# Products within a chunk of a bidirectional RWKV-7 scan: four 64x64 TensorE tiles in place of block-diagonal weights

## The chip, the core and the metric

The kernel runs as one program on one NeuronCore of a Trainium2 chip. The metric is the device time of one execution in microseconds (us). Three runs of the kernel before took 1759.25, 1768.68 and 1767.44 us; their median is 1767.44 us.

## The reference, cut to what matters

One layer mixes 128 context tokens and 2048 latent tokens. Eight heads of 64 channels go through RWKV-7 time mixing, once forwards and once backwards; the other half of the width is a short gated convolution. Projections stand before both and one output projection behind them. Only the scan matters here:

```python
def step(S, inp):
    r_t, w_t, k_t, v_t, kk_t, a_t = inp
    s_kk = jnp.einsum('bdhij,bdhj->bdhi', S, kk_t)
    S = (S * w_t[..., None, :] - s_kk[..., :, None] * (kk_t * a_t)[..., None, :]
         + v_t[..., :, None] * k_t[..., None, :])
    return S, jnp.einsum('bdhij,bdhj->bdhi', S, r_t)

s_final, ys = lax.scan(step, s0.astype(f32), xs)
ys = jnp.moveaxis(ys, 0, 2)
y = ys[:, 0] + jnp.flip(ys[:, 1], axis=1)
```

`S` is a 64x64 state for each head and direction. All of it is float32.

## The kernel before, in words

The kernel has three phases whose work overlaps. Phase 1 makes the projections (lines 158 to 160) and writes the scan's operands to memory. Phase 2 is the scan. Phase 3 is the output projection (lines 1219 to 1221).

**Chunks and stages.** The scan is done in chunks of 64 tokens. A pair of heads fills the 128 partitions, since each head has 64 channels. A stage (there are 17, `NST`) works on two groups, one for each direction (`gi` 0 and 1), and each group holds 8 units, a unit being one chunk of one head pair. For one unit the products between the chunk's own operands give four 64x64 blocks for each of the two heads.

**Parts of a stage.** `partL` loads the operands into `rr` (128 partitions: two heads of 64 channels; 5 operands; 8 units; 64 tokens). `partM` makes the products within a chunk: `F` (tile names `psF` in PSUM, `F` in SBUF) and `GA` (`psG`, `GA`), and `Q`, a transpose of one operand (`psQ`). `partI` inverts small triangular blocks on POOL. `partW`, `partU` and `partB` build from these the chunk's matrix `E`: `partU` with 32x32 matmuls (`psU`, `psW`), `partB` with 128x128 matmuls (`psX`, then `psE`). `partS` walks the eight steps of the state: a matmul `psS` of `E` with the state and values `sv`, and a scaling on VectorE that gives the next state. Stage `s`'s `partS` runs together with `partB` of stage `s+1` and `partM` of stage `s+3` (`LA = 3`).

**The products before.** A head pair lies on the 128 partitions, and the two heads must not mix. So `make_bd` (line 766) copies the weight operand into `bd`, a tile of zeros with one head's 64x64 block at the upper right and the other's at the lower left, and one 128x128 matmul gives both heads of one unit (line 829). A group needs two such tiles for each stage, each filled by two copies of 64x512 on ACT: 2 x 2 x 2 groups x 17 stages = 136 copies (line 716 is the helper `copy`). `F` and `GA` are made in halves of four units; a half fills one PSUM bank of 128x512 floats, and VectorE multiplies it by a mask on its way to SBUF (line 830). The pool `pm` has two such banks; `psF`, `psG` and `psQ` take turns in them.

**Slots.** In `F` and `GA` before, the slot number is the unit and the partition half is the head.

**What sets the order.** The code is recorded in the order in which `main` calls the parts. Then a scheduler of the framework goes over it with a timeline of its own and gives each engine a fixed order. TensorE, VectorE and the others run that order one after the other and wait on semaphores. Nothing is reordered between engines at run time by the program.

**How a float32 matmul shows in the trace.** A matmul of float32 is two passes: each is a weight load (PEld) and a matmul (PE) in the trace. So 272 matmuls for `psF` (17 stages x 2 groups x 8 units) show as x544.

## Time and profile before

| what | value |
|---|---|
| median of three runs | 1767.44 us |
| profiled execution, first to last instruction | 1770.7 us |
| PE busy, all matmuls (union) | 1649.1 us, 93% |
| PEld busy, weight loads | 1557.3 us, 88% |
| DVE (VectorE) busy | 1157.2 us, 65% |
| ACT (ScalarE) busy | 831.2 us, 47% |
| POOL (GpSimd) busy | 601.3 us, 34% |
| `psF` and `psG` matmul passes (line 829) | 544 + 544, union 79.7 + 74.7 us |
| copies into `bd` on ACT (line 716) | 136, 83.9 us |

The profiled execution gives no time of its own beside its span; the span is 3.3 us above the median of the runs. The products of `partM` run from 906.6 us to 1476.4 us of the span. A matmul's record in the trace is longer than what it keeps the array busy for, since matmuls are pipelined: the first record's start to the last record's start, divided by the steps between, gives the pace. A row of a timeline merges equal instructions that follow each other: it gives the start of the first, the time to the end of the last, and how many there are.

### The profile page before, as it was taken

How to read it: one execution, taken by the hardware profiler on the slowest of the kernel's cores; microseconds unless marked ns; L12 is line 12 of the kernel's file. 1: busy time of each engine (PE TensorE's matmuls, PEld its weight loads, DVE VectorE, ACT ScalarE, POOL GpSimd, SP SyncE). 2: the span in 40 equal slices, each digit the busy share in tenths (PEclk: the TensorE clock that was granted, in tenths of full speed). 3: DMA queues.
4: the chain of work that ended last, by engine and by line, in shares of the span. 5: the costliest groups of instructions: out<-in, count | busy, mean ns of one | idle time of the engine just before them, and what ended most of it. 6: DMA issues, size and time to landing. Idle time of an engine off the chain costs nothing. (4 is left out here: it accounts for less than half of the span.)

```text
span 1770.7 us, 33010 instructions
## 1 busy us (share of the span) xinstructions
PE 1649.1 (93%) x12400; PEld 1557.3 (88%) x12400; DVE 1157.2 (65%) x2197; ACT 831.2 (47%) x1607; POOL 601.3 (34%) x1089
## 2 busy tenths in 40 slices
PE   5999899999899999999999999899899899899998
PEld 3898899899888999999999989899799899787786
DVE  5998897545777635478843466777677677556333
ACT  4565544224454312255522177667567576433222
POOL 0132210001122100022205528877767868223221
PEclk9999999999899999999999989999899899899999
DMA  9788786564788743478776376767667784645432
GB/s 363 218 244 241 231 253 244 200 237 127 167 193 184 207 153 128 152 191 218 243 249 209 127 178 170 167 178 193 158 172 197 166 193 115 177 149 192 155 129 104
DMA packets 315376, 335.16 MB, mean 189 GB/s; under 512 B 166920, under 2 KB 263560, under 8 KB 301136
## 3 DMA queue, kind: packets, MB, share of 16 engines
q1 hardware_dynamic: 242912, 323.99, 61.5%
q10 hardware_dynamic: 70944, 4.60, 3.0%
q0 software_dynamic: 1360, 4.46, 0.7%
q8 instruction: 98, 1.61, 0.4%
q14 instruction: 62, 0.51, 0.1%
HBM read 221.16 MB, written 111.82 MB: 188 GB/s over the span
## 5 line engine op out<-in xcount | busy, mean ns | idle before, releaser
L871 POOL TENSOR_TENSOR zt<-zt,ztmp 128x30 f32<-128x30 f32 (+7 forms) x510 | 201.9, 396 | 39.7
L987 PE MATMUL psS<-sv,E 128*128 128x64 f32 x1088 | 153.1, 273 | 2.7 <-DVE sv L1000 2.5
L947 PE MATMUL psE<-str,stl 128*128 128x128 f32 x1088 | 149.3, 283 | 5.6 <-ACT str L714 3.8
L987 PEld LDWEIGHTS psS<-sv,E 128*128 128x128 f32 x1088 | 143.3, 197 | 5.9 <-DVE sv L1000 4.3
L947 PEld LDWEIGHTS psE<-str,stl 128*128 128x128 f32 x1088 | 135.0, 196 | 6.9 <-ACT str L714 4.6
L868 POOL TENSOR_TENSOR ztmp<-ab,zt 128x60 f32<-128x60 f32 (+7 forms) x255 | 132.4, 519 | 19.4
L716 ACT COPY bd<-rr 64x512 f32<-64x512 f32 x136 | 83.9, 617 | 90.2 <-issue 35.1
L314 POOL TENSOR_TENSOR shk<-rawl 128x384 f32<-128x384 f32 (+1 forms) x24 | 20.1, 838 | 277.1 <-ACT rawl L310 271.3
L948 DVE TENSOR_TENSOR E<-psE,msk 128x512 f32<-128x512 f32 x136 | 93.4, 687 | 24.3 <-PE psE L947 22.2
L936 PE MATMUL psX<-F,zb 128*128 128x128 f32 x544 | 79.6, 299 | 18.4 <-DVE E L948 13.2
L1000 DVE TENSOR_TENSOR sv<-psS,pc 64x128 f32<-64x128 f32 x254 | 67.9, 277 | 37.3 <-PE psS L987 35.6
L936 PEld LDWEIGHTS psX<-F,zb 128*128 128x128 f32 x544 | 71.8, 209 | 21.7 <-DVE E L948 16.1
L158 PE MATMUL mmv<-h,w 128*128 128x384 f32 (+1 forms) x192 | 70.1, 365 | 19.2 <-ACT q1r L312 10.1
L1282 POOL TENSOR_TENSOR z<-z,x 128x512 f32<-128x512 f32 x32 | 43.7, 1367 | 129.0 <-DVE z L1278 106.8
L829 PE MATMUL psF<-rr,bd 128*128 128x128 f32 x544 | 79.7, 294 | 2.7 <-ACT bd L716 1.8
L829 PE MATMUL psG<-rr,bd 128*128 128x128 f32 x544 | 74.7, 283 | 4.8 <-DVE F L830 4.8
L829 PEld LDWEIGHTS psF<-rr,bd 128*128 128x128 f32 x544 | 71.8, 206 | 3.3 <-issue 2.9
L829 PEld LDWEIGHTS psG<-rr,bd 128*128 128x128 f32 x544 | 68.3, 198 | 5.1 <-DVE F L830 5.0
L195 POOL TENSOR_TENSOR hsls<-sq,hshs 128x384 fp32r<-128x384 f32 (+1 forms) x24 | 31.6, 1318 | 109.5 <-DMA scr_vt<-vt 36.5
L159 PE MATMUL mmv<-h,w 128*128 128x384 f32 (+1 forms) x192 | 68.5, 357 | 0.0
L160 PE MATMUL mmv<-h,w 128*128 128x384 f32 (+1 forms) x192 | 68.0, 354 | 0.1
L158 PE MATMUL mmg<-h,w 128*128 128x384 f32 (+1 forms) x192 | 63.4, 330 | 4.0 <-ACT ta L374 2.0
(308 smaller groups left out, 5193.2 us busy)
## 6 DMA issues: line engine op xcount, KB each, us to landing
w<-scr_wsp SPq DMA_DIRECT2D x68, 1024.0 KB, 6.6
scr_wsp<-w SPq DMA_DIRECT2D x34, 1024.0 KB, 5.6
rr<-scr_ops SPq DMA_DIRECT2D x64, 512.0 KB, 5.0
scr_ops<-sp SPq DMA_DIRECT2D x160, 192.0 KB, 5.1
wr<-in_win SPq DMA_DIRECT2D x34, 512.0 KB, 7.5
ab<-scr_at SPq DMA_DIRECT2D x34, 256.0 KB, 3.8
x<-in_x SPq DMA_DIRECT2D x17, 512.0 KB, 3.7
wadas<-in_wada SPq DMA_DIRECT2D x8, 1024.0 KB, 15.2
```

The source lines that it names most:

```text
L158: T.matmul(ps[:, :n], w[:, 0, k], hh[:, 0, k, :n], start=k == 0, stop=False)
L159: T.matmul(ps[:, :n], w[:, 0, k], hh[:, 1, k, :n], start=False, stop=False)
L160: T.matmul(ps[:, :n], w[:, 1, k], hh[:, 0, k, :n], start=False, stop=k == 7)
L716: (V.tensor_copy if k in ON_DVE else P.copy)(dst, src)
L829: T.matmul(ps[:, i, :].rearrange("p (a b) -> p a b", b=64), w[:, u, :], x[:, :, u, :], start=True, stop=True)
L868: G.tensor_tensor(tv, ab[:, j:j + 2, j + 2:32].unsqueeze(1).broadcast_to((128, kn, 2, n)), zt[:, :kn, j:j + 2].unsqueeze(3).broadcast_to(( ...
L871: G.tensor_tensor(zt[:, :kn, j + 2:32], zt[:, :kn, j + 2:32], tv[:, :, r], ALU.subtract)
L936: T.matmul(px[:, i, :], B.zb[:, gi, us.start + i, :], g.F[:, us.start + i, :], start=True, stop=True)
L947: T.matmul(pe[:, i, hd, :].rearrange("p (b t) -> p b t", b=2), g.lt[:, :, hd, us.start + k + i].rearrange("p b t -> p (b t)"), g.rt[:, :, ...
L948: V.tensor_tensor(g.E[n][:, k:k + 2].rearrange("p a b c -> p (a b) c"), pe[:].rearrange("p a b c -> p (a b) c"), B.msk[:, ME[g.d]].unsquee ...
L987: T.matmul(sp[gi][:, q, hd, :], g.E[n][:, k, hd, :], sv[:, u, hd, :], start=True, stop=True)
L1000: r = V.tensor_tensor(dst, sp[gi][0:64, q], B.pc[0:64, d, 2 * p:2 * p + 2, c:c + 1].broadcast_to((64, 2, 64)), ALU.mult)
```

## The change

The block-diagonal tiles and their copies go. Each head's product of one chunk becomes a matmul of its own with 64 rows and 64 columns of weights, at one of four places in the array: its rows are the head's partitions (0 to 63 or 64 to 127), its columns are the half of the output partitions, and that half is now the parity `e` of the chunk. So four matmuls (two heads, two chunks) stand where two stood. A head's results go to a bank of their own: `ps[0]` for the first head, `ps[1]` for the second. `F` and `GA` are no longer made in halves: both banks are taken at once, 16 matmuls are recorded, and then both masks. In `F` and `GA` the slot number is now `4 * head + chunk pair` and the partition half is the chunk's parity. The operands that `partB` reads (`stl`, `str`) get a leading index for the half of the units, and the copies into them pick every second unit, with as many elements as before; `psX` takes its slots in the new order.

```diff
-MORD = ("Ff", "GgD", "", "Q")
+MORD = ("F", "GD", "", "Q")
...
-        B.bd = ring(O.r1, 2, [128, 8, 128], "bd", zero)
...
-        lt = ring(O.l1, 2, [128, 2, 8, 128], "stl", lambda t_: presetS(vl(t_)))
-        rt = ring(O.l1, 2, [128, 2, 2, 8, 64], "str", presetS)
+        lt = ring(O.l1, 2, [128, 2, 2, 4, 128], "stl", lambda t_: presetS(vl(t_)))
+        rt = ring(O.l1, 2, [128, 2, 2, 2, 4, 64], "str", presetS)
...
-    def make_bd(t_, src):
-        copy("b", t_[0:64, :, 64:128], src[0:64])
-        copy("c", t_[64:128, :, 0:64], src[64:128])
...
-            pb, qb = B.bd(), B.bd()
-            make_bd(pb, rr[:, 0])
-            make_bd(qb, rr[:, 4])
...
-            def product(h, dst, w, x, mask, nm):
-                ps = O.pm.tile([128, 4, 128], F32, tag="m", name=f"ps{nm}{s}_{gi}_{h}")
-                for i in range(4):
-                    u = h * 4 + i
-                    T.matmul(ps[:, i, :].rearrange("p (a b) -> p a b", b=64), w[:, u, :], x[:, :, u, :], start=True, stop=True)
-                V.tensor_tensor(dst[:, h * 4:h * 4 + 4, :], ps[:], mask.unsqueeze(1).broadcast_to((128, 4, 128)), ALU.mult)
+            def product(dst, w, x, mask, nm):
+                ps = [O.pm.tile([128, 4, 128], F32, tag="m", name=f"ps{nm}{s}_{gi}_{h}") for h in range(2)]
+                for a in range(4):
+                    for h, hr_ in enumerate((H0, H1)):
+                        for e, er in enumerate((H0, H1)):
+                            u = 2 * a + e
+                            T.matmul(ps[h][er, a, :].rearrange("p (a b) -> p a b", b=64), w[hr_, u, :], x[hr_, :, u, :], start=True, stop=True)
+                for h in range(2):
+                    V.tensor_tensor(dst[:, h * 4:h * 4 + 4, :], ps[h][:], mask.unsqueeze(1).broadcast_to((128, 4, 128)), ALU.mult)
...
-            F = lambda h: product(h, g.F, pb, rr[:, 2:4], B.msk[:, MF[d]], "F")
-            GA = lambda h: product(h, g.GA, qb, rr[:, 1::-1], B.mkg[:, MG[d]], "G")
+            F = lambda: product(g.F, rr[:, 0], rr[:, 2:4], B.msk[:, MF[d]], "F")
+            GA = lambda: product(g.GA, rr[:, 4], rr[:, 1::-1], B.mkg[:, MG[d]], "G")
...
-                for i in range(4):
-                    T.matmul(px[:, i, :], B.zb[:, gi, us.start + i, :], g.F[:, us.start + i, :], start=True, stop=True)
+                k = us.start // 2
                 for hd in range(2):
-                    copy("x" if hd else "y", g.fs[64:128, :, hd, us], px[64 - hd * 64:128 - hd * 64].rearrange("p u (b t) -> p b u t", b=2), True)
+                    for a in range(2):
+                        v = hd * 4 + k + a
+                        T.matmul(px[:, hd * 2 + a, :], B.zb[:, gi, v, :], g.F[:, v, :], start=True, stop=True)
+                for e in range(2):
+                    copy("x" if e else "y", g.fs[64:128, :, us.start // 4].rearrange("p b h u t -> p b (h u) t")[:, :, e:8:2], px[e * 64:e * 64 + 64].rearrange("p u (b t) -> p b u t", b=2), True)
```

The order on TensorE changes with it. First the place where `F` of the last stage's first group (`psF16_0`) stands, before. The last number of the name is the half of the units; `x4` is four matmuls in a row.

```order
L822 MATMUL psQ15_1_15458<-idt2_8815,rr1_8836 128x128 x4
L829 MATMUL psF16_0_0_15676<-rr0_8835,bd0_8831 128x128 x4
L910 MATMUL psU13_15355<-zr_1455_15312,GA10_8826 32x32 x16
L910 MATMUL psU13_15355<-zr_1455_15312,GA11_8829 32x32 x16
L987 MATMUL psS12_0_4_15450<-sv_1425_14762,E_1448_15192 128x64 x2
L987 MATMUL psS12_1_4_15454<-sv_1426_14771,E_1449_15200 128x64 x2
L829 MATMUL psF16_0_1_15682<-rr0_8835,bd0_8831 128x128 x4
```

And the same product after, where the last number of the name is the head, and `64x128` is the output of one tile:

```order
L824 MATMUL psF16_0_0_16060<-rr0_8831 64x128 x5
L934 MATMUL psX13_0_0_15861<-F10_8825,zb_10067 128x128 x2
...
L934 MATMUL psX13_1_0_15869<-F11_8828,zb_10067 128x128 x4
L824 MATMUL psF16_0_1_16061<-rr0_8831 64x128 x3
L985 MATMUL psS12_0_4_15838<-sv_1425_15102,E_1448_15556 128x64 x2
L824 MATMUL psF16_0_1_16061<-rr0_8831 64x128
L985 MATMUL psS12_1_4_15842<-sv_1426_15111,E_1449_15564 128x64 x2
L824 MATMUL psF16_0_0_16060<-rr0_8831 64x128
L824 MATMUL psF16_0_1_16061<-rr0_8831 64x128
L945 MATMUL psE13_0_00_15876<-str0_10056,stl0_10046 128x128 x4
L824 MATMUL psF16_0_1_16061<-rr0_8831 64x128
```

Two pieces of four matmuls became pieces of five, three, one, two and more, with 128x128 matmuls between them, and the scheduler put the first head's matmuls ahead of the second's. Over the whole program the order has 1088 matmuls of 64x64 tiles in 151 such pieces.

Second, TensorE at `GA` of the same stage's other group (`psG16_1`), before:

```order
L829 MATMUL psG16_1_0_15747<-rr1_8836,bd1_8832 128x128 x4
L947 MATMUL psE13_0_11_15638<-str0_10008,stl0_10002 128x128 x4
L987 MATMUL psS13_0_0_15664<-sv_1445_15178,E_1463_15472 128x64 x2
L947 MATMUL psE13_1_11_15644<-str1_10009,stl1_10003 128x128 x4
L829 MATMUL psG16_1_1_15753<-rr1_8836,bd1_8832 128x128 x4
```

and after:

```order
L824 MATMUL psF16_1_1_16132<-rr1_8832 64x128 x2
L905 MATMUL psU14_16175<-zr_1477_16120,GA20_10032 32x32 x16
L905 MATMUL psU14_16175<-zr_1477_16120,GA21_10035 32x32 x16
L985 MATMUL psS13_0_0_16052<-sv_1445_15542,E_1463_15860 128x64 x2
L985 MATMUL psS13_1_0_16056<-sv_1446_15551,E_1464_15868 128x64 x2
L824 MATMUL psG16_1_0_16151<-rr1_8832 64x128 x8
L824 MATMUL psG16_1_1_16152<-rr1_8832 64x128 x8
```

Here the product stands in one piece of 16, eight of one head and then eight of the other, and between it and the end of `psF16_1` stand 32 small matmuls and four of the state.

Third, VectorE at the masks of that group's `F` and `GA`, after:

```order
L946 TENSOR_TENSOR E_1473_16006<-psE13_1_11_16032,msk_8805 128x512
L715 COPY stl1_10047<-GA21_10035 64x4x64
L826 TENSOR_TENSOR F11_8828<-psF16_1_0_16131,msk_8805 128x512
L826 TENSOR_TENSOR F11_8828<-psF16_1_1_16132,msk_8805 128x512
L998 TENSOR_TENSOR sv_1445_15542<-psS13_0_0_16052,pc_10043 64x128
L998 TENSOR_TENSOR sv_1446_15551<-psS13_1_0_16056,pc_10043 64x128
L826 TENSOR_TENSOR GA11_8829<-psG16_1_0_16151,mkg_8806 128x512
```

Before, the two masks of one `F` stood apart, with `E` masks and state scalings between them; now they follow each other, since both heads' matmuls end together.

More of the change, by code (lines that the diff above doesn't have):

```diff
@@ L726, in vl @@
     def vl(t_):
-        return t_[:].rearrange("p h u (b t) -> p b h u t", b=2)
+        return t_[:].rearrange("p f h u (b t) -> p b f h u t", b=2)
     def presetS(t_):
-        for hd in range(2):
-            V.tensor_copy(t_[0:64, 0, hd], B.I2[0:64].unsqueeze(1).broadcast_to((64, 8, 64)))
+        for f in range(2):
+            for hd in range(2):
+                V.tensor_copy(t_[0:64, 0, f, hd], B.I2[0:64].unsqueeze(1).broadcast_to((64, 4, 64)))
     def tl(shape, tag, b, pool=None, dt=F32):
@@ L776, in load_stk @@
         for i in range(4 // n):
-            dst = t_[0:64, 1, :, us.start + n * i:us.start + n * (i + 1)]
+            dst = t_[0:64, 1, us.start // 4, :, n * i:n * (i + 1)]
             x = src[(p + i) * 128:(p + i + 1) * 128, c0 * 64:(c0 + n) * 64]
@@ L885, in partW @@
                 for i in range(2):
-                    r = slice(64 - i * 64, 128 - i * 64)
-                    copy("g", g.gs[64:128, 1, i, us], g.GA[r, us, 0:64])
                     k = us.start // 2
-                    copy("h", g.gs[64:128, 0, :, us.start + i:us.stop:2], g.Q[i * 64:i * 64 + 64, k:k + 2].rearrange("p k (h c) -> p h k c", h=2))
+                    copy("g", g.gs[64:128, 1, us.start // 4, :, i:4:2], g.GA[i * 64:i * 64 + 64].rearrange("p (h a) t -> p h a t", h=2)[:, :, k:k + 2, 0:64])
+                    copy("h", g.gs[64:128, 0, us.start // 4, :, i:4:2], g.Q[i * 64:i * 64 + 64, k:k + 2].rearrange("p k (h c) -> p h k c", h=2))
                 if n == 0:
@@ L946, in partB @@
                         for hd in range(2):
-                            T.matmul(pe[:, i, hd, :].rearrange("p (b t) -> p b t", b=2), g.lt[:, :, hd, us.start + k + i].rearrange("p b t -> p (b t)"), g.rt[:, :, hd, us.start + k + i], start=True, stop=True)
+                            T.matmul(pe[:, i, hd, :].rearrange("p (b t) -> p b t", b=2), g.lt[:, :, us.start // 4, hd, k + i].rearrange("p b t -> p (b t)"), g.rt[:, :, us.start // 4, hd, k + i], start=True, stop=True)
                     V.tensor_tensor(g.E[n][:, k:k + 2].rearrange("p a b c -> p (a b) c"), pe[:].rearrange("p a b c -> p (a b) c"),
```

2 lines of the change are left out of this document (1 added, 1 removed).

## The prediction

> **What bounds the kernel now.** I read the page's busy times first, then the busy times by stretch, then one stage's groups and its timeline on TensorE, and last the waits.
>
> ```profile
> PE 1649.1 (93%) x12400; PEld 1557.3 (88%) x12400; DVE 1157.2 (65%) x2197; ACT 831.2 (47%) x1607; POOL 601.3 (34%) x1089
> ```
>
> ```profile
> core 0: us, PE busy (x) PEld busy (x) DVE busy (x) ACT busy (x) POOL busy (x), PEclk, DMA share, GB/s
> 1050.00:1480.00 430.00, 404.62 (x4882) 394.10 (x4882) 315.73 (x669) 292.33 (x534) 328.26 (x722) 0.97 0.70 173
> 1185.90:1215.70 29.80, 29.50 (x367) 28.74 (x366) 22.00 (x49) 23.11 (x43) 23.35 (x52) 1.00 0.78 195
> ```
>
> PE is the busiest engine, and it is so in the scan (1050 to 1480 us) and in one whole stage of it (1185.9 to 1215.7 us). The next engine, POOL, has 6 us of slack in that stage. But a PE that shows as busy isn't yet a PE at its limit, so I price the stage by pace. Its groups, and pieces of its timeline on PE (start, us, what, how many):
>
> ```profile
> L987 PE MATMUL psS<-sv,E 128*128 128x64 f32 x64 | 8.8, 267 | 0.0
> L947 PE MATMUL psE<-str,stl 128*128 128x128 f32 x64 | 8.7, 279 | 0.0
> L829 PE MATMUL psF<-rr,bd 128*128 128x128 f32 x32 | 4.4, 280 | 0.0
> L829 PE MATMUL psG<-rr,bd 128*128 128x128 f32 x32 | 4.3, 277 | 0.0
> L936 PE MATMUL psX<-F,zb 128*128 128x128 f32 x32 | 4.2, 278 | 0.3 <-DVE E L948 0.3
> L822 PE MATMUL psQ<-idt,rr 128*128 128x128 f32 x9 | 1.7, 275 | 0.0
> L1065 PE MATMUL psT<-idt,y 128*128 128x128 f32 x4 | 0.7, 286 | 0.0
> ```
>
> ```profile
> 1184.14 1.06 PE L829 MATMUL psG<-rr,bd 128*128 128x128 f32 x8
> ...
> 1185.86 1.20 PE L910 MATMUL psU<-zr,GA 32*32 32x32 f32 x64
> 1186.99 1.10 PE L987 MATMUL psS<-sv,E 128*128 128x64 f32 x8
> ...
> 1188.94 0.56 PE L987 MATMUL psS<-sv,E 128*128 128x64 f32 x4
> 1189.43 0.24 PE L917 MATMUL psW<-zc,bu 32*32 32x32 f32 x2
> 1189.60 0.66 PE L987 MATMUL psS<-sv,E 128*128 128x64 f32 x4
> ```
>
> Eight passes of `psG` take 1.06 us; one lasts 0.277 in the group, so the pace is (1.06 - 0.277) / 7 = 0.112 us a pass. `psS`, with half the columns to stream, is no faster (1.10 us for eight), so a pass costs its weight load of 128 columns as much as its stream of 128. The 32x32 passes run on two tiles of the array: 64 in 1.20 us, a last one of 0.19 taken off, is 0.016 a pass, or 0.032 on each tile.
>
> The last three rows give the price of leaving the full array and coming back. The first four `psS` end at 1189.50, the next four at 1190.26. Four passes need 0.45, so 0.31 went to the excursion, of which the two `psW` passes on one tile are 0.06: **0.25 us a round trip**.
>
> The stage has 64 + 64 + 32 + 32 + 32 + 8 + 4 = 236 full passes (one of the nine `psQ` belongs to the stage before): 26.4 us. Its 128 small passes are 2.0, and its 5 changes of mode, 2.5 round trips, 0.6. That is 29.0 of 29.8 us: such a stage is limited by PE, and what the change adds to PE or takes from it goes to the time nearly one for one. Where PE still waits:
>
> ```profile
> PE psX L936 <- DVE E L948: 12.1, 12, 3.8
> PE psQ L822 <- DVE GA L830: 7.6, 1, 7.6
> PE psS L987 <- DVE sv L1000: 2.0, 5, 0.7
> PE psE L947 <- DVE E L948: 1.7, 1, 1.7
> PE psW L917 <- ACT bu L716: 0.9, 1, 0.9
> PE psF L829 <- DVE y L1017: 0.7, 1, 0.7
> ```
>
> These are 25.0 us between 1050 and 1480: all that could absorb more work on PE there.
>
> **The change, part by part.**
>
> *Removed: full-array passes.* `psF` and `psG` are 544 + 544 passes:
>
> ```profile
> L829 PE MATMUL psF<-rr,bd 128*128 128x128 f32 x544 | 79.7, 294 | 2.7 <-ACT bd L716 1.8 <-DVE y L1017 0.7 <-ACT Q L716 0.2
> L829 PE MATMUL psG<-rr,bd 128*128 128x128 f32 x544 | 74.7, 283 | 4.8 <-DVE F L830 4.8
> L716 ACT COPY bd<-rr 64x512 f32<-64x512 f32 x136 | 83.9, 617 | 90.2 <-issue 35.1 <-PE psF L829 26.0 <-PE psG L829 12.8
> ```
>
> By pace they take 1088 x 0.112 = 121.9 us (the unions, 154, count the tails that lie beside other matmuls).
>
> *Added: passes on 64x64 tiles.* 2176 of them, twice as many, each still with 128 columns to stream: I take 0.112 a pass on its own tile. No row shows a 64x64 tile. What is near is `psrow`, phase 1's product on four column tiles that share all 128 rows, 512 columns streamed. Its passes by stretch:
>
> ```profile
> core 0: us, PE busy (x) PEld busy (x) DVE busy (x), PEclk, DMA share, GB/s
> 34.40:34.48 0.08, 0.02 (x4) 0.03 (x4) 0.00 (x0) 1.00 1.48 614
> 34.48:34.90 0.42, 0.42 (x4) 0.13 (x8) 0.00 (x0) 1.00 0.86 351
> 34.90:34.94 0.04, 0.04 (x8) 0.00 (x0) 0.00 (x0) 1.00 0.52 192
> ```
>
> Four passes start within the first 0.08 us and four more only after 34.90; all eight weight loads are under way by then. So four tiles stream together though they share their rows, and each tile's second pass waits at its own tile without holding back the next tile. With four tiles always at work the 2176 passes would be 544 steps, 60.9 us. The order doesn't give that: the 151 pieces are short, and many run one head's two tiles first (`psG16_1_0` x8, then `psG16_1_1` x8). Counting for each piece the passes on its fullest tile gives 838 steps, 93.9 us, if tiles run ahead freely; with room for just one waiting pass at each tile (all that `psrow` shows) it is 936 steps, 104.8 us. So this term is **-28.0 to -17.1 us**; I take -22, the middle, since neither depth is shown.
>
> *Added: changes of mode.* Counted in the order, the array leaves full width 52 times before and 155 times after, and changes straight between 64x64 and 32x32 39 times. 103 more round trips at 0.25 are 25.8 us. A 64-column first load is longer than a 32-column one by a quarter of 0.112, 0.028, and where a 128-column product follows in place of `psS` its stream adds half of 0.112, 0.056: 0.33 at most, 34.0 us. The 39 direct changes at half a round trip add 4.9 to 6.4. Together **+31 to +40 us**; I take +36, as most pieces end before `psE`, not `psS`.
>
> *Removed: 136 copies on ACT*, 83.9 us there. PE waited for `bd` 1.8 us in all and for ACT otherwise 0.9 us in the scan: credited at nothing, since ACT isn't what PE waits for; at most -3.
>
> *Moved: masks.* 136 masks before and after, of the same size (0.69 us by the row below), but both banks of `pm` are now held until both masks are done.
>
> ```profile
> L830 DVE TENSOR_TENSOR F<-psF,msk 128x512 f32<-128x512 f32 x68 | 46.4, 684 | 28.7 <-PE psF L829 15.0 <-PE psX L936 13.1
> ```
>
> What waits is the next product's first matmul, and behind it everything on PE. In the second place shown above, 32 small matmuls and four of `psS` (1.0 + 0.9 us and two half trips) cover the two masks (1.4 us) and what VectorE has ahead of them (a mask of `E` and a copy, 1.1 us, begun when `psE` ended a product earlier). So nothing is charged. Without that cover a product waits up to 1.4 us, at 34 places `F` then `GA`.
>
> *The rest.* `psX`, the copies into `stl` and `str` and all DMAs keep their number and size: nothing, hidden or not. Four presets more at the start of the scan, of half the size: nothing.
>
> **Sum.** -22 + 36 = +14 us (bounds -28 + 31 = +3 and -17 + 40 = +23). On the profiled 1770.7 that is 1784.7; the median of the runs is 3.3 lower, so **1781 us**, with its own range 1770 to 1791.
>
> [...]
>
> **The rivals.**
>
> A. *The drains fall into waits PE has anyway.* The pieces of one or two matmuls stand where the scheduler saw room, so they may sit in the 25.0 us. If all of it is absorbed: 14 - 25 = -11, 1756 us; with the best bound, 3 - 25 = -22, 1745. It turns to faster by over 0.5% (8.8 us, about what a measurement can tell from no change) when 23 of the 25 us are absorbed, or 12 at the best bound. Against it: the longest waits are few (7.6 is one event) and lie at a mask, not at a product.
>
> B. *Passes stay in strict order.* Then the pieces take 1239 steps, 138.8 us: +17 instead of -22, and with the changes of mode +53: 1820 us.
>
> C. *Two tiles on the same rows take turns.* Then only the two heads overlap: with one waiting pass 1802 steps, 201.8 us, +80 + 36 = +116: 1883 us. `psrow` speaks against it, though there no two row groups are at work.
>
> D. *The two banks make a new wait.* Half of the 34 places uncovered, at 1.4 us, adds 24: 1805 us; all of them, 48: 1829 us.
>
> **How the numbers follow.** Forecast 0.56, of which 0.14 lies within 8.8 us of 1767.4 (sums below +9) and 0.42 above; A 0.19, faster; B 0.06; C 0.04; D 0.15, all three slower. Faster 0.19, same 0.14, slower 0.67. The range 1748 to 1822 leaves out C, half of A's lower end and the tops of B and D, under 0.2 in all.
>
> **What would show it.** Right: `psF` and `psG` have 2176 passes, 64x128; in a piece of eight on one head, two end together every 0.112 us; a `psS` before and after a piece is 0.25 to 0.33 us further apart than its passes explain; a stage's full passes number about 172; the stages of the scan are 30.5 to 31.5 us where they were 29.8 to 31.0; ACT loses some 84 us, and the time doesn't show it. Wrong: PE's waits before `psG` on the `F` masks grow past 10 us (D), or PE's total wait in the scan falls under 10 us (A), or sixteen passes of one piece take 1.8 us and more (B, C).

## The result, and the profile after

The changed kernel takes **1837.68 us** (median of 4, 1825.81 to 1838.91), the kernel before, run beside it, 1768.06: a ratio of 1.038, 95% interval 1.0351 to 1.0409. By that ratio it is some 67 us more (the medians differ by 69.6) where 14 were forecast. The direction was right, the size was not. The profiled execution has a span of 1835.3 us.

The page's busy times after:

```profile
PE 1685.3 (92%) x13488; PEld 1553.3 (85%) x13488; DVE 1151.2 (63%) x2205; ACT 748.4 (41%) x1471; POOL 595.1 (32%) x1087
```

ScalarE has lost 82.8 us, TensorE gained 36 us. That TensorE's sum grew so little while the time grew by 67 says that part of the loss is not work. The busy times by stretch (columns as in the prediction: stretch, length, the engines' busy times, granted clock, DMA share and rate):

```profile
1050.00:1480.00 430.00, 390.16 (x4988) 350.58 (x4988) 266.65 (x579) 196.72 (x368) 283.72 (x630) 0.90 0.64 151
1209.60:1240.40 30.80, 30.67 (x432) 27.71 (x428) 21.90 (x48) 18.19 (x34) 18.78 (x43) 1.00 0.74 174
```

The second row is one undisturbed stage, from its first `psU` to the next. It takes 30.8 us where one took 29.8: inside the 30.5 to 31.5 that the prediction gave. The first row holds the rest: the granted clock is 0.90 where it was 0.97, and although the clock is lower TensorE is busy for less of the stretch (390 of 430 us, 404 before).

The whole scan can be divided the same way. Take the time from the first `psF` pass to the last `psS` pass, subtract the time in which no matmul record runs (waits), and from the rest half of what lies in stretches at half clock (what the clock lost; in m1 below full passes start 0.213 us apart at half clock and 0.112 at full). What is left is the work, as it would be at full clock. Before, 698.9 us are 625.9 of work, 26.6 lost to the clock and 46.3 of waits; after, 766.0 are 637.6, 55.4 and 73.0. So the change cost 12 us of work, 29 of clock and 27 of waits. The work is what was forecast at 14.

Where the waits come from shows on SyncE's queue between 1050 and 1480 us. The kernel before:

```profile
SPq L851 <- DMA scr_at<-dg: 61.4, 13, 6.5
SPq L896 <- DMA scr_zt<-zt: 46.0, 11, 7.4
```

and after, where L847 is the load of `ab` and L891 that of `zc`:

```profile
SPq L891 <- DMA scr_zt<-zt: 106.8, 9, 17.0
SPq L847 <- DMA scr_at<-dg: 8.7, 2, 5.4
```

The queue now stands for up to 17 us at the load of `zc`, which needs GpSimd's stored `zt`, and no longer at the load of `ab`. The reason is the order in which SyncE issues (the program's order of its DMAs, cut to one stage; `x2` is two in a row). Before:

```
L805 DMA rr_8836<-scr_ops_59 128x2x512 x2
L851 DMA ab_12654<-scr_at 64x1024 x2
L1038 DMA sg_12828<-scr_sg 128x512
L1074 DMA scr_mixT<-yo_12572 128x512
L896 DMA zc_12731<-scr_zt 64x16x32 x2
```

and after:

```
L801 DMA rr_8832<-scr_ops_59 128x2x512
L891 DMA zc_12519<-scr_zt 64x16x32 x2
L847 DMA ab_12442<-scr_at 64x1024 x2
L1036 DMA sg_12628<-scr_sg 128x512
L1072 DMA scr_mixT<-yo_12360 128x512
L801 DMA rr_8832<-scr_ops_59 128x2x512
```

No line of the diff touches these loads; the scheduler placed them anew. What it does at one stage is seen in the timelines of SyncE's queue, GpSimd, VectorE and TensorE after (start, us, what, and in brackets the idle time before it and what ended it):

```profile
1144.55 0.61 POOL L868 DMA_DIRECT2D scr_zt<-zt  x1 [0.30 <-POOL zt L867]
1147.05 1.32 SPq L891 DMA_DIRECT2D zc<-scr_zt  x2
1148.47 1.25 SPq L847 DMA_DIRECT2D ab<-scr_at  x2
1151.81 0.72 SPq L977 DMA_DIRECT2D sv<-in_st  x1
1153.93 0.20 POOL L856 COPY dgp<-ab 128x16 f32<-128x16 f32 x1 [6.12 <-DMA ab<-scr_at]
1159.76 0.28 DVE L979 TENSOR_REDUCE mn<-sv 64x2 f32<-64x128 f32 x1 [7.73 <-DMA sv<-in_st]
1160.29 1.12 PE L985 MATMUL psS<-sv,E 128*128 128x64 f32 x4 [7.37 <-DVE sv L998]
```

GpSimd ends one `zt`, and only when that has landed does SyncE get past `zc` and issue the `ab` that GpSimd needs for the next one: 9.4 us from its store to its first operation on that `ab`. The last two rows are another wait: TensorE waits for VectorE, and VectorE for `st0` (the load `sv<-in_st`, the first state of a head pair), which stands behind `zc` on the queue as well; theory 3 below is about that load.

Before, the `ab` was issued ahead, and these are 6.2 us apart, most of them the landing of the store:

```profile
1255.61 1.11 SPq L851 DMA_DIRECT2D ab<-scr_at  x2
1257.72 0.62 POOL L872 DMA_DIRECT2D scr_zt<-zt  x1 [0.30 <-POOL zt L871]
1262.94 0.53 POOL L856 MEMSET zt<- 128x512 f32 x1 [4.60 <-DMA scr_zt<-zt]
1263.03 1.34 SPq L896 DMA_DIRECT2D zc<-scr_zt  x2
1263.87 0.21 POOL L860 COPY dgp<-ab 128x16 f32<-128x16 f32 x1
```

The third and the sixteenth of GpSimd's 17 stores of `zt`, first before, then after:

```profile
1075.57 0.62 POOL L872 DMA_DIRECT2D scr_zt<-zt  x1 [0.30 <-POOL zt L871]
...
1487.27 0.62 POOL L872 DMA_DIRECT2D scr_zt<-zt  x1 [0.30 <-POOL zt L871]
```

```profile
1072.03 0.61 POOL L868 DMA_DIRECT2D scr_zt<-zt  x1 [0.30 <-POOL zt L867]
...
1548.39 0.61 POOL L868 DMA_DIRECT2D scr_zt<-zt  x1 [0.30 <-POOL zt L867]
```

Thirteen stages in 411.7 us, 31.7 each, against 476.4 us, 36.6 each: 65 us in all, nearly the whole difference. That GpSimd's loop is now as long as the kernel's pace doesn't by itself say which holds which; the experiments do. TensorE still does most stages in 30 to 35 us, and pays at every fourth or so, where the head pair changes (42 to 53 us).

What it pays there is more than the wait. After the wait shown above, by stretch:

```profile
1152.90:1160.30 7.40, 0.03 (x2) 0.01 (x1) 0.54 (x3) 3.67 (x7) 5.53 (x12) 0.70 1.04 204
1160.30:1176.40 16.10, 16.10 (x86) 14.32 (x88) 9.32 (x23) 2.30 (x5) 13.94 (x28) 0.50 0.25 68
1176.40:1185.00 8.60, 8.60 (x227) 7.72 (x226) 7.79 (x15) 2.77 (x6) 4.31 (x13) 1.00 0.70 192
```

and around a wait of the same length (7.6 us idle) at such a stage before:

```profile
1262.40:1271.40 9.00, 1.37 (x13) 1.23 (x12) 1.53 (x4) 1.31 (x5) 7.35 (x16) 0.69 0.78 175
1271.40:1275.90 4.50, 4.31 (x19) 3.91 (x20) 4.28 (x12) 2.54 (x5) 3.94 (x8) 0.50 1.04 257
1275.90:1285.60 9.70, 9.70 (x88) 9.58 (x87) 8.04 (x18) 6.93 (x13) 8.37 (x18) 1.00 0.22 53
```

In both kernels the clock is at half after the wait. Before, it is full again after 4.5 us of work; after, TensorE works for 16.1 us without a pause before it is.

### The profile page after: what moved, and what is told of

It is laid out like the page before. It is cut to its first block, busy times and chain, and to the rows that moved or that the text cites. A ratio compares the mean times of both kernels' runs of the same rounds, so it can differ in the third digit from the quotient of the medians.

```text
span 1835.3 us, 35161 instructions
## 1 busy us (share of the span) xinstructions
PE 1685.3 (92%) x13488; PEld 1553.3 (85%) x13488; DVE 1151.2 (63%) x2205; ACT 748.4 (41%) x1471; POOL 595.1 (32%) x1087
## 5 line engine op out<-in xcount | busy, mean ns | idle before, releaser
L945 PE MATMUL psE<-str,stl 128*128 128x128 f32 x1088 | 158.9, 294 | 22.4 <-DVE E L946 21.4
L985 PE MATMUL psS<-sv,E 128*128 128x64 f32 x1088 | 159.0, 283 | 8.3 <-DVE sv L998 8.3
L985 PEld LDWEIGHTS psS<-sv,E 128*128 128x128 f32 x1088 | 148.3, 204 | 16.1 <-DVE sv L998 9.8
L934 PE MATMUL psX<-F,zb 128*128 128x128 f32 x544 | 86.2, 307 | 7.6 <-DVE E L946 3.7
L158 PE MATMUL mmv<-h,w 128*128 128x384 f32 (+1 forms) x192 | 68.0, 354 | 18.7 <-ACT q1r L312 10.6
L824 PE MATMUL psF<-rr 64*64 64x128 f32 x1088 | 75.1, 300 | 10.3 <-DMA rr<-scr_ops 5.6
L824 PE MATMUL psG<-rr 64*64 64x128 f32 x1088 | 72.0, 295 | 6.9 <-DVE F L826 6.9
L824 PEld LDWEIGHTS psF<-rr 64*64 64x64 f32 x1088 | 52.1, 145 | 21.3 <-issue 4.4
L824 PEld LDWEIGHTS psG<-rr 64*64 64x64 f32 x1088 | 55.7, 143 | 13.7 <-DVE F L826 7.4
L160 PE MATMUL mmv<-h,w 128*128 128x384 f32 (+1 forms) x192 | 66.4, 346 | 0.1
L159 PE MATMUL mmv<-h,w 128*128 128x384 f32 (+1 forms) x192 | 66.2, 345 | 0.0
L195 POOL TENSOR_TENSOR hsls<-sq,hshs 128x384 fp32r<-128x384 f32 (+1 forms) x24 | 30.0, 1252 | 107.9 <-ACT hshs L194 31.7
L158 PE MATMUL mmc<-h,w 128*128 128x384 f32 (+1 forms) x192 | 64.2, 335 | 0.5 <-DMA w<-scr_wsp 0.5
```

Source lines behind the costliest of these rows:

```text
L158: T.matmul(ps[:, :n], w[:, 0, k], hh[:, 0, k, :n], start=k == 0, stop=False)
L159: T.matmul(ps[:, :n], w[:, 0, k], hh[:, 1, k, :n], start=False, stop=False)
L160: T.matmul(ps[:, :n], w[:, 1, k], hh[:, 0, k, :n], start=False, stop=k == 7)
L824: T.matmul(ps[h][er, a, :].rearrange("p (a b) -> p a b", b=64), w[hr_, u, :], x[hr_, :, u, :], start=True, stop=True)
L934: T.matmul(px[:, hd * 2 + a, :], B.zb[:, gi, v, :], g.F[:, v, :], start=True, stop=True)
L945: T.matmul(pe[:, i, hd, :].rearrange("p (b t) -> p b t", b=2), g.lt[:, :, us.start // 4, hd, k + i].rearrange("p b t -> p (b t)"), g.rt[:, ...
```

## The experiments

Three theories of what the forecast missed: (1) the queue's order lengthens GpSimd's loop; (2) the clock, once it has fallen, stays down because of the new tiles; (3) the load of `st0`, on which VectorE waits at the head-pair boundaries, starts the loss. Ratios are to the kernel before, run beside each; differences of two ratios are turned into us with 1767.

**The queue's order, put back and put in (e1, e2).** e1 is the changed kernel, with one more order among SyncE's loads and nothing else (a `NoSync` dependency sets which of two instructions of an engine is issued first, and waits for nothing):

```
-            D(ab[h * 64:h * 64 + 64].rearrange("p j i -> p (j i)"), at.rearrange("u s b j i -> (u s b) (j i)"))
+            O.ab[s] = D(ab[h * 64:h * 64 + 64].rearrange("p j i -> p (j i)"), at.rearrange("u s b j i -> (u s b) (j i)"))
...
-                    D(st.zc[h:128:2], S["zt"][s][h].rearrange("u s b q i -> (s b q) u i"))
+                    z = D(st.zc[h:128:2], S["zt"][s][h].rearrange("u s b q i -> (s b q) u i"))
+                    if s + 1 in O.ab:
+                        tc.add_manual_dep(z.ins, O.ab[s + 1].ins.name, mybir.DependencyInfo(mybir.DependencyClass.NoSync, mybir.DependencyReason.DATA), reason="order")
```

> The changed kernel with one order put back on SyncE's queue: the loads of zc of one stage are issued after the loads of ab of the next (as they are in the kernel before), where the changed kernel has zc first. TensorE's order is untouched. Theory 1 (the queue's order makes GpSimd's chain zt, zc, ab, zt a serial loop, so zt and the st0 loads come late and TensorE waits at the head-pair boundaries): about 40 us back, 1785 to 1800 us, the boundary stages back near 39 us from 47 to 53, GpSimd's wait for ab below 120 us from 166. Theory 2 (the granted clock falls and stays low because of the pieces on 64x64 tiles themselves): within 10 us of the changed kernel, 1828 to 1848, and the time at half clock stays above 120 us. Theory 3 (the st0 load in VectorE's order): little change, 1825 to 1848, VectorE still waits some 31 us for sv.

Measured: 1801.82 us, ratio 1.0185 (1.0151 to 1.0219): 34 us back. TensorE, VectorE and ScalarE run the same operations in the same order as in the changed kernel, and GpSimd does but for two short places, so SyncE's order is worth the 34 us by itself. GpSimd's stores of `zt` are 34.6 us apart, where they were 36.6 and before 31.7. SyncE's waits are nearly those of before:

```profile
SPq L848 <- DMA scr_at<-dg: 54.0, 11, 6.0
SPq L892 <- DMA scr_zt<-zt: 33.0, 8, 6.1
```

e2 is the kernel before with the opposite edit: the loads of `ab` and GpSimd's part are recorded after the next stage's `zc` and ordered behind it.

> The kernel before (block-diagonal weights, full-array products) with the queue's order of the changed kernel: each stage's loads of ab, and the part on GpSimd that they feed, are put behind the loads of zc of the stage before. Nothing of TensorE's work changes. Theory 1: 30 to 50 us slower than before, 1798 to 1818 us, with the added time at the stages where the head pair changes. Theories 2 and 3: within 10 us of before, 1758 to 1778.

Measured: 1858.58 us, ratio 1.0497 (1.0467 to 1.0527): 88 us, more than expected. Here TensorE waits for the transposed `zt` nine times:

```profile
PE psU L913 <- DVE zr L905: 28.4, 9, 6.2
```

No tile of that kernel differs from before, so a late `ab` costs without any change of tiles. How much of the 88 us is SyncE's order is open: GpSimd's part moved too, and with it TensorE's order, which is not that of before. e1 is the clean test (e16 below is another). Theory 1 stands; it doesn't explain the 1802 of e1.

**The structure alone (e4).** The kernel before, still with block-diagonal weights, with each product recorded whole, both banks taken and both masks behind:

```
-MORD = ("Ff", "GgD", "", "Q")
+MORD = ("F", "GD", "", "Q")
...
+                ps = [O.pm.tile([128, 4, 128], F32, tag="m", name=f"ps{nm}{s}_{gi}_{h}") for h in range(2)]
+                for h in range(2):
+                    for i in range(4):
+                        u = h * 4 + i
+                        T.matmul(ps[h][:, i, :].rearrange("p (a b) -> p a b", b=64), w[:, u, :], x[:, :, u, :], start=True, stop=True)
+                for h in range(2):
+                    V.tensor_tensor(dst[:, h * 4:h * 4 + 4, :], ps[h][:], mask.unsqueeze(1).broadcast_to((128, 4, 128)), ALU.mult)
```

> The kernel before with only the structure of its products changed as in the changed kernel: a product is issued whole (both banks of pm taken, eight full-array passes, then the two masks), still with block-diagonal weights; the queue's order stays that of before. If the masks and the two banks make the wait: 15 to 50 us slower, 1783 to 1818, with TensorE waiting for F and GA before psG and psQ. If the loss lies in the tiles, the queue or the clock: within 10 us of before, 1758 to 1778.

Measured: 1766.35 us, ratio 0.9987 (0.9962 to 1.0012). This shows less than it was meant to: in the trace every compute engine runs the same operations in the same order as before, so the scheduler kept each product in halves and only the recording differs. Whether two banks at once cost the changed kernel anything shows in its own waits between 900 and 1650 us:

```profile
PE psG L824 <- DVE F L826: 6.9, 3, 6.1
PE psQ L815 <- DVE GA L826: 6.5, 2, 5.6
```

Before, these are 4.8 and 7.6 us: the two together have grown by 1 us.

**The load of `st0` (e3, e7, e10, e11, e9, then e14, e13).** e3 issues it with the stage's `sv` loads in the changed kernel; e7 does the same on top of e1.

> The changed kernel with the st0 loads moved ahead: they are issued with the stage's sv loads, one stage earlier, in place of right before VectorE's mean of them. Theory 3 (that load in VectorE's order starts the loss at each boundary): VectorE's wait for sv goes from some 31 us to under 5 and 25 to 45 us come back, 1793 to 1813. Theory 1 alone: zt still comes late, at most 10 us back, 1828 to 1838. Theory 2 alone: no change beyond the waits themselves, 1828 to 1842.

> The changed kernel with the queue's order put back and the st0 loads one stage earlier; products in pieces as in the changed kernel. Theory 3 in its weaker form (the loads are late only in part because of zc; the rest is their own place): 8 to 25 us under the run with ab first, 1777 to 1794. Otherwise 1796 to 1808, the rest of its loss (34 us over before, of which the changes of mode explain 14 and the clock some 19) standing as it is.

Measured: e3 1844.19 us (1.0453, 1.039 to 1.0515); e7 1801.12 (1.0191, 1.0142 to 1.0241). No gain, but the wait was not gone: in e3 the load stood behind `zc` as the `sv` loads do.

```profile
DVE mn L980 <- DMA sv<-in_st: 22.0, 3, 8.7
```

e10 (changed kernel), e11 (e1) and e9 (before) load it three stages early into a tile of its own.

```
+        if st.g[0].blk == 1 and st.g[0].units[0][0] < 3:
+            for d in range(2):
+                D(B.s0[d][:], A["st0"][:, d, p0:p0 + 2, :])
```

> The changed kernel with the st0 loads three stages ahead, its queue's order as it was. Theory 3 (the load in VectorE's order makes the loss): 25 to 45 us under the changed kernel, 1793 to 1813. Theory 1 (GpSimd's loop over zc and ab is what is late, the load only the last link): at most 15 us under it, 1823 to 1838.

> The changed kernel with the queue's order put back and the st0 loads three stages ahead. With both waits gone, what is left over before is the changes of mode (+14 by the forecast) and the clock's slower return after the waits that remain: 1780 to 1795 us. If it stays near the run with ab first (1802), the load had no part in the loss.

> The kernel before with the same st0 loads three stages ahead. It says what of the joined kernel's gain is the load's alone: before waits 14.7 us for it between 1050 and 1480 us, so 10 to 25 us under before, 1742 to 1757, if the wait reaches TensorE; within 5 us if it is hidden.

Measured: e10 1837.41 us (1.0356, 1.0295 to 1.0417), e11 1795.79 (1.0157, 1.0124 to 1.0191), e9 1765.03 (0.9987, 0.9964 to 1.0011). Again inconclusive. The scheduler put VectorE's mean of `st0` right behind the earlier load, so VectorE, which works in order, now waited there:

```profile
DVE mn L986 <- DMA s<-in_st: 14.8, 2, 11.4
```

So e14 and e13 add one order: the mean is queued behind the last scaling of the state.

```
+                        r = V.tensor_reduce(mn[:], x0, mybir.AxisListType.X, ALU.add)
+                        if O.scaled is not None:
+                            tc.add_manual_dep(r.ins, O.scaled.name, mybir.DependencyInfo(mybir.DependencyClass.NoSync, mybir.DependencyReason.DATA), reason="order")
```

> The changed kernel with the two edits on st0, its queue's order as it was: VectorE's wait for st0 (18.8 us in three with the early load alone) goes away in truth. Theory 3: 25 to 45 us under the changed kernel, 1793 to 1813. Theory 1 (what is late is zt, from GpSimd's loop): at most 15 us under it, 1823 to 1838.

> The kernel before with the same two edits on st0. If the wait for st0 costs the kernel before what it shows (13.9 us in five): 8 to 20 us under before, 1748 to 1760, the boundary stages at 33 to 36 us in place of 39. If it is hidden: within 5 us.

Measured: e14 1828.08 us (1.0344, 1.0311 to 1.0378), e13 1758.07 (0.9949, 0.993 to 0.9968). No wait for `in_st` is left on VectorE in either. It was worth some 6 us in the changed kernel and 9 before (each ratio is known to 0.2 to 0.3%, 3 to 6 us), so theory 3 falls as a cause of the difference.

**The clock by itself (m1).** The kernel keeps nothing of the computation. `wait` is 20 copies on VectorE into the tile that TensorE reads next, and `done` a copy of the results:

```
    for f in STRETCHES:
        wait()
        {"f": full, "n": narrow, "2": two, "4": four, "t": turn, "s": small, "m": mix}[f[0]](int(f[1:]))
        full(64)
        done()
```

> Leaves the whole computation out and measures the clock by itself: seven times TensorE waits some 20 us for VectorE and then runs without a wait: 128 full-array matmuls; 256 on two 64x64 tiles of one head; 512 on four 64x64 tiles in turn; 512 on four, one head's eight first, then the other's; 1024 on two 32x32 tiles; 128 full-array ones with 64 columns; and 4 full-array ones and 8 on two 64x64 tiles alternately; after each, 64 full-array ones. If the granted clock follows the share of the array that works (as the stretches at half clock of all runs suggest: those with the weight of 13 full passes in 3.4 us end, those under 11 do not): half clock ends within 7 us in the first and third, and stays half through the second and the fifth until the full-array ones come. If it follows only whether TensorE is busy: half clock ends within 7 us in all seven. Paces expected at full clock: 0.112 us a full pass, 0.112 a step of two tiles, the same for four in turn; eight of one head first between that and twice that.

Measured, the stretches by their own windows: full passes; two 64x64 tiles; four in turn; eight of one head, then eight of the other; two 32x32 tiles; full arrays with 64 columns; four full matmuls and eight on two tiles alternately. A matmul is two passes.

```profile
20.28:64.75 44.47, 44.47 (x384) 44.28 (x384) 0.69 (x1) 0.00 (x0) 1.00 0.00 1
79.97:134.78 54.81, 54.81 (x513) 54.48 (x513) 0.00 (x0) 0.00 (x0) 0.50 0.00 1
166.62:196.36 29.74, 29.74 (x1025) 29.57 (x1025) 0.00 (x0) 0.00 (x0) 0.95 0.02 4
226.06:261.05 34.99, 34.99 (x1025) 34.82 (x1025) 0.00 (x0) 0.00 (x0) 0.92 0.02 4
290.76:349.09 58.33, 56.52 (x2049) 55.52 (x2049) 0.00 (x0) 0.00 (x0) 0.50 0.02 4
381.25:436.13 54.88, 54.88 (x257) 54.88 (x258) 0.00 (x0) 0.00 (x0) 0.50 0.00 1
467.37:529.87 62.50, 62.50 (x384) 53.63 (x384) 0.00 (x0) 0.00 (x0) 0.50 0.00 1
```

TensorE has no pause in them, the short ones in the fifth (1.8 of 58 us) apart, and yet the clock came back only in the three stretches that, by the weights below, have the most of the array at work: in the third (0.95 over its 29.74 us), in the fourth (0.92 over 34.99), and in the first (its record starts late, so that the row reads 1.00, but its first twelve passes are 0.213 us apart and the later ones 0.112). On two 64x64 tiles it stayed at half for 54.8 us, on full arrays with 64 columns for 54.9, and with full passes between two tiles (last row) for 62.5 us. After the four at half it came back 3.4 to 5.2 us after the full passes that follow had begun. So in m1 being busy was not enough (54.81 of 54.81 us at 0.50), and the share of the array at work told the stretches apart. Theory 2 stands.

The scan's stretches agree. The shortest stretch at half clock in the records is 3.41 us. I cut every half-clock stretch between 900 and 1620 us of six runs (before, after, e1 to e4) into pieces of that length and gave each pass the share of the array that it streams: a full pass 1, `psS` with its 64 columns 1/2, a 64x64 pass 1/4, a 32x32 one 1/64. Of 120 pieces under 11, one was followed by full clock; of 35 from 11 to 13, 21; of 48 from 13 up, 46. Seven runs that played no part in finding the bounds (e5 and e12 to e17) give 0 of 123, 16 of 40 and 61 of 62. A stage of the kernel before weighs 172 + 64/2 + 128/64 = 206; at half clock its 29 us are 58, 17 pieces, 12.1 each. A stage after weighs 108 + 32 + 128/4 + 2 = 174, over 61 us 9.7 each. By this estimate the old stage climbs out by itself, and the new one gets out only where full passes bunch.

**Products in one piece (e5, e6, e8, e12).** To have four tiles at work at once, e5 takes e1, makes the two banks one tile, so that a product starts when both are free, and chains its matmuls at a high priority.

```
-                ps = [O.pm.tile([128, 4, 128], F32, tag="m", name=f"ps{nm}{s}_{gi}_{h}") for h in range(2)]
+                ps = O.pm.tile([128, 2, 4, 128], F32, tag="m", bufs=1, name=f"ps{nm}{s}_{gi}")
+                with tc.high_priority():
...
+                                r = T.matmul(ps[er, h, a, :].rearrange("p (a b) -> p a b", b=64), w[hr_, u, :], x[hr_, :, u, :], start=True, stop=True)
+                                if last is not None:
+                                    tc.add_manual_dep(r.ins, last, NOSYNC, reason="order")
+                                last = r.ins.name
```

> The changed kernel with the queue's order put back (as in the run with ab first) and each product in one piece: both banks are one tile, so a product starts when both are free, and its 32 passes go out together with the four tiles taking turns. Products 544 steps of 0.112 us, 60.9 us, in place of 121.9 in the kernel before and 94 to 105 in the changed one; the array leaves full width 88 times where it did 52 before (155 in the changed kernel) and changes directly 23 times: 36 x 0.25 to 0.33 plus 23 x 0.13 to 0.17, 12 to 16 us. If the passes set the time: 45 to 49 us under before, less what the masks hold back, 1725 to 1760 us, and 45 to 75 us under the run with ab first (1802). If the wait for both banks takes the gain (68 products that wait up to 1.4 us each): 1780 to 1830, with TensorE waiting for F and GA above 40 us. If four tiles do not stream together: 1800 or more, a piece of 32 passes taking 1.8 us or more.

> The run with joined products, and the st0 loads issued one stage earlier with the sv loads. If the st0 load starts a loss at the boundaries once the queue is in order: 5 to 25 us under the run with joined products alone, VectorE's wait for sv from some 11 to under 3 us. If not: within 6 us of it.

> The run with joined products, and st0 for the next head pair loaded into a small tile of its own three stages before it is needed, so that VectorE never waits for that load. VectorE's wait for it (10 to 30 us in three or four waits) goes to zero. If that wait is what starts the loss at the boundaries: TensorE's waits of 5 to 8 us for F, GA and E there go with it and the clock stays up, 15 to 35 us under the run with joined products (1774), 1739 to 1759. If something else is as late at the boundary: within 8 us of it.

> The run with joined products and early st0 loads, and VectorE's mean of st0 is queued behind the last scaling of the state of the stage before, in place of right behind its load, three stages early, where the scheduler had put it. VectorE's wait for in_st (13.3 us) goes to under 2 us. If that wait starts the loss at the boundaries: the boundary stages go from some 39 us to 33 to 36, half clock between 900 and 1620 us from 119 to under 90, 15 to 35 us under the run before it (1766), 1731 to 1751. If the boundary's loss comes from elsewhere: within 8 us.

Measured: e5 1773.95 us (1.003, 1.0005 to 1.0056); with the `st0` edits of e3, e10 and e14, e6 1765.36 (0.9999, 0.9975 to 1.0022), e8 1766.16 (0.9994, 0.9975 to 1.0013) and e12 1755.36 (**0.9932**, 0.991 to 0.9954). A product of 32 passes takes 1.10 us in e5's timeline on TensorE, as long as eight full passes in a row (1.06 before), so four tiles do stream together:

```profile
1186.34 1.10 PE L829 MATMUL psF<-rr 64*64 64x128 f32 x32
```

Joining is worth 27 us over e1, not the 45 to 75 expected. In e5 between 1050 and 1480 us the clock is 0.92 and TensorE idle for 39 us, 14 more than before:

```profile
1050.00:1480.00 430.00, 390.54 (x5792) 364.58 (x5791) 308.81 (x667) 227.10 (x426) 321.66 (x714) 0.92 0.68 174
```

Divided as above, e5's scan of 700.7 us is 580.8 of work, 48.2 lost to the clock and 71.7 of waits. So the passes fell by the 45 us that were expected, and the clock (22 us more than before) and the waits (25 more) took them back.

e12 is faster than both kernels, but the kernel before with the same `st0` edits (e13, 0.9949) isn't told apart from it.

**What is left for the tiles (e15), the order again (e16), GpSimd's loop (e17).** e15 is the changed kernel with the orders of e1 and of e14. e16 is e12 without the order of e1, which puts `zc` first again; TensorE, VectorE and ScalarE run in the same order as in e12. e17 is e12 with GpSimd's clearing of the next `zt` moved behind its first copy out of `ab`, so that it doesn't wait for its own store:

```
-        G.memset(zt[:], 0.0)
...
-        G.tensor_copy(dg[:], ab[:].rearrange("p j i -> p (j i)")[:, 1:1024:66])
+        c = G.tensor_copy(dg[:], ab[:].rearrange("p j i -> p (j i)")[:, 1:1024:66])
+        r = G.memset(zt[:], 0.0)
+        tc.add_manual_dep(r.ins, c.ins.name, NOSYNC, reason="order")
```

> The changed kernel with both delays out of the way: zc behind ab on SyncE's queue, st0 early and VectorE's mean of it in its place. What is left over the kernel before with the same st0 edits (1758) is the change of tiles itself, in its pieces: by the forecast's sum +14 (3 to 23), 1761 to 1781, with the clock's slower return up to 1795. If the queue's order and st0 were not the causes: near 1802.

> The joined kernel with st0 late, but with the queue's order of the changed kernel (zc ahead of ab); TensorE's order is the same. If the queue's order costs by itself, whatever the tiles: 25 to 45 us over the joined kernel with ab first (1755), 1780 to 1800, with SyncE's wait at zc for zt near 100 us. If the queue mattered only with products in pieces: within 10 us of 1755.

> The joined kernel with ab first and st0 late (1755 us), and GpSimd's clearing of the next zt queued behind its first copy out of ab, in place of right behind the store of the zt before, where it waits 1.8 to 4.5 us a stage for that store to land. GpSimd's loop is 27 to 28 us of work a stage and this wait; its stores of zt come 31 us apart on average in the joined kernel, as the stages do. If this loop is what the joined kernel is held to (and so where its 40 to 50 us of saved passes went): the stores come 28 to 29.5 us apart and the time falls by 20 to 40 us, 1715 to 1735. If TensorE or the clock hold it: within 8 us of 1755, and GpSimd waits for ab in place of the store.

Measured: e15 1795.9 us (1.0168, 1.0099 to 1.0236), e16 1816.44 (1.0283, 1.0246 to 1.032), e17 1760.53 (0.9956, 0.993 to 0.9982). e16 is 62 us over e12, with this wait on SyncE's queue:

```profile
SPq L902 <- DMA scr_zt<-zt: 176.2, 12, 19.0
```

e15 is 39 us over e13. The stretch from 900 to 1620 us, before, after, e13 and e15:

```profile
900.00:1620.00 720.00, 671.61 (x7042) 645.71 (x7042) 466.50 (x978) 401.21 (x734) 433.60 (x918) 0.96 0.66 175
```

```profile
900.00:1620.00 720.00, 648.58 (x7677) 591.89 (x7675) 418.18 (x910) 293.77 (x550) 413.23 (x907) 0.91 0.62 160
```

```profile
900.00:1620.00 720.00, 679.58 (x7079) 650.49 (x7079) 479.75 (x990) 404.49 (x742) 435.22 (x920) 0.97 0.66 178
```

```profile
900.00:1620.00 720.00, 682.33 (x8002) 621.63 (x8001) 446.90 (x954) 308.12 (x573) 417.47 (x911) 0.93 0.64 168
```

Divided as above, from the first `psF` to the last `psS`, in us:

| run | scan | work at full clock | lost to the clock | waits |
|---|---|---|---|---|
| before | 698.9 | 625.9 | 26.6 | 46.3 |
| after | 766.0 | 637.6 | 55.4 | 73.0 |
| e1 (after, order put back) | 733.5 | 638.5 | 51.0 | 44.0 |
| e13 (before, `st0` early) | 688.6 | 629.0 | 21.3 | 38.2 |
| e14 (after, `st0` early) | 755.5 | 639.8 | 73.5 | 42.1 |
| e15 (e14, order put back) | 728.2 | 643.4 | 47.4 | 37.4 |
| e12 (joined, `st0` early) | 682.3 | 587.2 | 35.1 | 60.0 |
| e16 (e12, `zc` first) | 741.1 | 579.2 | 69.2 | 92.7 |

These are single executions. With SyncE's order as before, the tiles cost 13 us of work and 24 of clock (e1 against before), or 14 and 26 (e15 against e13), and no waits. The order costs 29 us of waits and 4 of clock between after and e1; between e14 and e15 it is 5 and 26. So the time that a late `zt` takes from TensorE can show as a wait or as work at half clock.

e17 gave nothing: the wait for the store is gone, and GpSimd waits for `ab` instead.

```profile
POOL dgp L863 <- DMA ab<-scr_at: 48.7, 11, 9.9
```

So the wait for the store alone doesn't hold the joined kernel. Against e13, e12 has 42 us less of work, but lost 14 us more to the clock and waits 22 us longer. What makes these waits is left open: the path from `GA` through `scr_at` to `ab` was not taken apart there.

## Why the prediction was right or wrong

**The failed step** is "`psX`, the copies into `stl` and `str` and all DMAs keep their number and size: nothing". Their number and size did stay; their order did not. `zc` went ahead of `ab` on SyncE, and that is 34 us of the 67 (the changed kernel less e1; 31 by e14 less e15), some three times what the sum's bounds allowed on either side. The prediction compared the order on TensorE and VectorE and not on SyncE.

**A second step failed with it**: "The next engine, POOL, has 6 us of slack in that stage". GpSimd's idle time stood in a loop in which each `zt` waits for the store of the last and for `ab`, and the stores came 31.7 us apart, as far as the stages. In the stage shown, the changed order put 3.2 us into that loop (9.4 for 6.2); the stores then came 36.6 us apart, and putting the order back alone (e1) gave 34 us. So the 6 us were not there to be used up without cost. Whether GpSimd held the pace in the kernel before is not shown.

**A third was left out.** Every pass was priced at full clock. By the weights above the tiles halve that of the products, and a wait after which the clock was at half for 4.5 us of work was followed by 16.1. That is 24 us of the 35 by which e1's scan is longer than that of before, and 26 of the 40 between e15 and e13. No term or rival of the forecast held it. m1 shows the clock go with the share of the array at work (0.50 on two tiles, 0.95 on four in turn), and so do the weighed pieces; no run gave the changed kernel the old weight with all else kept.

**Right in its terms.** *Passes and changes*, +14 (bounds +3 to +23): the work rose by 12 us (after against before), 13 (e1) and 14 (e15 against e13), and the undisturbed stage is 30.8 us. In such a stage 172 full passes (19.3 us) and the small ones (2.0) leave 9.5 for the products and the changes; by the forecast's terms for one of 17 stages, the products are 99.9/17 = 5.9 and the some ten round trips at 0.3 are 3. *The round trip*: between four `psS` at 1220.89 and the next four at 1221.83 stand the two passes of one matmul, one after the other on one tile, and two changes, (0.94 - 6 x 0.112) = 0.27, inside the 0.25 to 0.33:

```profile
1220.89 0.66 PE L985 MATMUL psS<-sv,E 128*128 128x64 f32 x4
1221.47 0.43 PE L824 MATMUL psF<-rr 64*64 64x128 f32 x2
1221.83 0.66 PE L985 MATMUL psS<-sv,E 128*128 128x64 f32 x4
```

*ScalarE's copies*: 82.8 us gone there (84 forecast), and the time doesn't show it.

**The rivals.** A (drains hidden) fell: the time went up. B (strict order) fell: in m1 eight matmuls of one head before eight of the other, on four tiles, took 34.99 us in all, some 5.6 of it at half clock (0.92 over the row), where one head after the other would be, by an estimate, 512 steps of 0.107, 54.9 (0.107 is half of the 0.214 that a step of two tiles took in m1's second row at half clock). So the waiting passes of one head's tiles did not hold back the other's there. C (two tiles on the same rows take turns) fell by m1's third row: 256 steps of four tiles in 29.7 us, some 3 us of it at half clock (0.95 over the row). In the changed kernel itself a whole product of 32 passes takes 1.11 us, where eight full passes took 1.06 before:

```profile
1176.92 1.11 PE L824 MATMUL psF<-rr 64*64 64x128 f32 x32
```

D (two banks) fell by the changed kernel's own waits: 6.9 us before `psG` on the masks of `F`, under the 10 that it asked for; that its 1805 to 1829 came near the time was luck.

**The range**, 1748 to 1822, left out what happened, because it was made of TensorE's terms alone. The direction would have come out right by the 12 us of work; of the other 55 us the forecast held nothing.

## What to carry to other kernels

Where a scheduler orders the program, a change of one engine's work reorders the queues of all: compare the order on every engine that issues loads, and ask of each load which wait it now stands behind. An engine that is idle inside a loop of store, load and work may have no slack; time its loop, not only its busy share. And before a full-array product is cut into small tiles, count what a stage weighs per 3.41 us at half clock, the shortest such stretch in these records. In this kernel, where that fell from some 12 full passes to under 10, a wait of 7.4 us was followed by 16.1 us at half clock, which is 8 us more lost.

## What the runs showed of the hardware

- In m1 the granted clock went with the share of the array at work, not with TensorE's being busy: two 64x64 tiles ran 54.81 of 54.81 us without a pause at 0.50, and so did full passes with 64 columns (54.88 us); on four 64x64 tiles in turn the clock came back (0.95 over 29.74 us), as it did on full passes (0.213 us apart for the first twelve, then 0.112). The shortest stretch at half clock in the records of the scan is 3.41 us.
- The falls need not be more to cost more: between 900 and 1620 us, e15 has 7 stretches at half clock of 102 us in all, e13 has 10 of 44 us.
- A load moved to an early place in a program can make the wait for it move along: in e10 VectorE's operation was scheduled right behind it and waited up to 11.4 us there, three stages ahead of need. An order on the waiting operation (e14) took the wait away.
